# Channel shuffle on one core: one VectorE copy a tile in place of a VectorE and ScalarE pair, and a new list of tile sizes

## The chip, the cores and the metric

One core of a Trainium2 chip. The metric is the device time of one execution in microseconds (us), as a median over several executions.

## The reference

```python
# x: (16, 64, 64, 256) float32, groups = 8
x = x.reshape(batch, h, w, groups, c // groups)
x = x.transpose(0, 1, 2, 4, 3)          # inside each row of 256 channels: 8 x 32 -> 32 x 8
return x.reshape(batch, h, w, c)
```

Each of the 65,536 rows of 1 KB is permuted in itself. 67.11 MB are read and as many written; there is no arithmetic.

## The kernel before

A tile has 128 partitions, and each partition holds q consecutive rows, so "a 24 KB tile" means 24 KB a partition, 3.146 MB in all. In the memory of the chip a partition's part of a tile is one contiguous run of q KB. I call such a run a *row of the transfer* below. A transfer *lands* when its last bytes have arrived and the engine that waits for it can go on. The *plateau* is the flat rate in the middle of a run.

```python
_SIZES = [24] * 21 + [8]
_IN_BUFS = 4
_OUT_BUFS = 4
_SHARES = (("vector", 1), ("scalar", 1))
...
for q in _SIZES:
    in_tile = in_pool.tile([P, biggest * c], F32, name="in_tile")
    nc.sync.dma_start(out=in_tile[:, : q * c], in_=rows(x_flat, first, q))       # load
    out_tile = out_pool.tile([P, biggest * c], F32, name="out_tile")
    ...  # half of the tile's rows to nc.vector.tensor_copy, half to nc.scalar.copy,
         # each permuting "p (i g j)" -> "p (i j g)"
    nc.scalar.dma_start(out=rows(out_flat, first, q), in_=out_tile[:, : q * c])  # store
    first += P * q
```

Loads are issued by the SP queue, stores by ScalarE's queue. Four input and four output buffers of 24 KB take 192 KB of each partition.

## Time and profile before

| | before |
|---|---|
| time, median | 317.7 us |
| span of the profile | 316.0 us |
| VectorE / ScalarE busy | 21% / 38% |
| bytes / 432 GB/s | 310.7 us |
| first landing / first store issued | 11.04 / 16.80 us |
| last landing / last bytes | 302.35 / 313.7 us |

The page of the profile is read from its DMA row. If that is at 9 in every slice and the load and store queues together take nearly all of the sixteen DMA engines, an engine's idle time only says that it waits for data. The question for any change is then which part of the 5.3 us above the floor of 310.7 it can reach. The prediction shows the lines.

### The profile page before, as it was taken

The page shows a single profiled execution, that of the slowest core. Times are in us where ns is not written, and L with a number is a line of the kernel's source. Part 1 is how long each engine was busy: PE and PEld are TensorE (multiplying, and loading weights), DVE is VectorE, ACT ScalarE, POOL GpSimd, SP SyncE. Part 2 cuts the span into 40 slices and gives each one's busy share as a digit, 9 for nine tenths or more (in the row PEclk, how much of TensorE's full clock was granted, in tenths as well). Part 3 has the DMA queues.
Part 4 walks back from the last instruction along what each step waited for, and adds up shares of the span by engine and source line. Part 5 has one row for each costly group of instructions (what it writes and reads, how often), then busy time and mean ns, then how long its engine had stood idle before and what let it go on. Part 6 is the DMA issues. An engine that isn't in the chain of part 4 may idle for free.

```text
span 316.0 us, 236 instructions
## 1 busy us (share of the span) xinstructions
DVE 65.3 (21%) x22; ACT 118.9 (38%) x23; POOL 0.2 (0%) x4
## 2 busy tenths in 40 slices
DVE  0440321303030303113030303031220303030310
ACT  1681624425160606243351606061533426060620
POOL 0000000000000000000000000000000000000000
DMA  8999999999999999999999999999999999999996
GB/s 302 439 395 426 426 445 432 420 442 439 417 439 445 417 436 442 426 426 445 426 423 445 439 414 442 442 417 439 442 421 432 442 420 432 442 429 429 421 446 291
DMA packets 6337, 134.23 MB, mean 425 GB/s; under 512 B 704, under 2 KB 704, under 8 KB 704
## 3 DMA queue, kind: packets, MB, share of 16 engines
q1 hardware_dynamic: 3168, 67.11, 49.8%
q10 hardware_dynamic: 3168, 67.11, 49.3%
q14 instruction: 1, 0.01, 0.0%
HBM read 67.11 MB, written 67.11 MB: 425 GB/s over the span
## 4 chain that ended last, share of the span: by engine, by line
another core or an unknown queue 43%; DMA 32%; ACT 20%; ACTq 1%; issue 0%
DMA in_tile<-in_x_dram 32%; ACT out_tile L49 20%; ACTq L66 1%; ACTq L49 0%
## 5 line engine op out<-in xcount | busy, mean ns | idle before, releaser
L49 ACT COPY out_tile<-in_tile 128x3072 f32<-128x3072 f32 (+1 forms) x22 | 117.7, 5348 | 184.6 <-DMA in_tile<-in_x_dram 184.6
L51 DVE COPY out_tile<-in_tile 128x3072 f32<-128x3072 f32 (+1 forms) x22 | 65.3, 2968 | 238.3 <-DMA in_tile<-in_x_dram 238.3
L49 ACT ACT_TABLE_LOAD x1 | 1.3, 1283 | 0.7 <-PEq L84 0.7
L84 POOL MEMSET const-bfloat16-1.0<- 128x1 bf16 x1 | 0.1, 102 | 0.0
L84 POOL MEMSET const-uint8-127<- 128x1 uint8 x1 | 0.1, 102 | 0.0
L84 POOL MEMSET const-float32-1.0<- 128x1 f32 x1 | 0.1, 99 | 0.0
L84 POOL MEMSET const-float32-0.0<- 128x1 f32 x1 | 0.1, 98 | 0.2 <-issue 0.2
## 6 DMA issues: line engine op xcount, KB each, us to landing
in_tile<-in_x_dram SPq DMA_DIRECT2D x21, 3072.0 KB, 52.6
out_dram<-out_tile ACTq DMA_DIRECT2D x21, 3072.0 KB, 20.2
in_tile<-in_x_dram SPq DMA_DIRECT2D x1, 1024.0 KB, 47.9
out_dram<-out_tile ACTq DMA_DIRECT2D x1, 1024.0 KB, 10.4
```

Of the source, the lines that this page charges most:

```text
L49: nc.scalar.copy(out=dst, in_=src)
L51: getattr(nc, engine).tensor_copy(out=dst, in_=src)
L66: nc.scalar.dma_start(out=rows(out_flat, first, q), in_=out_tile[:, : q * c])
L84: nc = _bacc.Bacc("TRN2", target_bir_lowering=False, num_devices=1)
```

## The change

The intent: let stores begin earlier (small tiles first), take ScalarE out of the copying so that it only issues stores, and keep everything in program order. 44 transfers become 48. The line with `manual_schedule` is meant to keep the program order; no run has it alone (e1 has it together with the VectorE copies, e2 has neither).

```diff
-_SIZES = [24] * 21 + [8]
+_SIZES = [4, 4, 8] + [24] * 20 + [16]
...
-_SHARES = (("vector", 1), ("scalar", 1))
...
+    ctx.enter_context(tc.manual_schedule(engines=None))
...
-        at, total = 0, sum(n for _, n in _SHARES)
-        for k, (engine, n) in enumerate(_SHARES):
-            ...
-            permute(engine, out_tile[:, cols], in_tile[:, cols])
+        nc.vector.tensor_copy(
+            out=out_tile[:, : q * c].rearrange("p (i j g) -> p i j g", j=CPG, g=G),
+            in_=in_tile[:, : q * c].rearrange("p (i g j) -> p i j g", g=G, j=CPG),
+        )
```

More of the change, by code (lines that the diff above doesn't have):

```diff
@@ L43, in rows @@
         return flat[first * c : (first + P * q) * c].rearrange("(p f) -> p f", p=P)
-    def permute(engine, dst, src):
-        src = src.rearrange("p (i g j) -> p i j g", g=G, j=CPG)
-        dst = dst.rearrange("p (i j g) -> p i j g", j=CPG, g=G)
-        if engine == "scalar":
-            nc.scalar.copy(out=dst, in_=src)
-        else:
-            getattr(nc, engine).tensor_copy(out=dst, in_=src)
+    ctx.enter_context(tc.manual_schedule(engines=None))
     first = 0
@@ L57 @@
         out_tile = out_pool.tile([P, biggest * c], F32, name="out_tile")
-        at, total = 0, sum(n for _, n in _SHARES)
-        for k, (engine, n) in enumerate(_SHARES):
-            last = k == len(_SHARES) - 1
-            upto = q if last else min(q, at + -(-q * n // total))
-            if upto > at:
-                cols = slice(at * c, upto * c)
-                permute(engine, out_tile[:, cols], in_tile[:, cols])
-            at = upto
+        nc.vector.tensor_copy(
+            out=out_tile[:, : q * c].rearrange("p (i j g) -> p i j g", j=CPG, g=G),
+            in_=in_tile[:, : q * c].rearrange("p (i g j) -> p i j g", g=G, j=CPG),
+        )
         nc.scalar.dma_start(out=rows(out_flat, first, q), in_=out_tile[:, : q * c])
```

## The prediction

> **What bounds the kernel now.** I read the page from the top: busy shares first, then the DMA rows, then the waits, then windows cut at the kernel's own events.
>
> ```profile
> DVE 65.3 (21%) x22; ACT 118.9 (38%) x23; POOL 0.2 (0%) x4
> ...
> DMA  8999999999999999999999999999999999999996
> ...
> q1 hardware_dynamic: 3168, 67.11, 49.8%
> q10 hardware_dynamic: 3168, 67.11, 49.3%
> ...
> L49 ACT COPY out_tile<-in_tile 128x3072 f32<-128x3072 f32 (+1 forms) x22 | 117.7, 5348 | 184.6 <-DMA in_tile<-in_x_dram 184.6
> L51 DVE COPY out_tile<-in_tile 128x3072 f32<-128x3072 f32 (+1 forms) x22 | 65.3, 2968 | 238.3 <-DMA in_tile<-in_x_dram 238.3
> ```
>
> The two copying engines work for 21% and 38% of the span of 316.0 us, and all their other idle time ends with the landing of an input tile. The load queue (q1) and the store queue (q10) together take 49.8 + 49.3 = 99.1% of what sixteen DMA engines have. In the row of forty slices only the first and the last are below 9. So the kernel is bound by the transfers, and what is left beside them is at the two ends. The next view says how much (windows cut at the landings of tiles 0 to 3, at the last two landings and at the last bytes; the last two columns are DMA share and GB/s):
>
> ```profile
> 0.00:2.00 2.00, 0.00 (x0) 1.27 (x1) 0.20 (x4) 1.00 0.71 160
> 2.00:18.30 16.30, 3.16 (x1) 5.74 (x2) 0.00 (x0) 1.00 0.96 410
> 18.30:30.80 12.50, 3.25 (x1) 5.86 (x1) 0.00 (x0) 1.00 1.00 405
> 30.80:60.00 29.20, 6.47 (x2) 11.71 (x3) 0.00 (x0) 1.00 1.00 433
> 60.00:292.60 232.60, 48.31 (x16) 86.99 (x16) 0.00 (x0) 1.00 1.00 432
> 292.60:302.40 9.80, 3.02 (x1) 5.48 (x2) 0.00 (x0) 1.00 1.05 450
> 302.40:313.70 11.30, 1.09 (x1) 1.89 (x1) 0.00 (x0) 1.00 0.96 411
> 313.70:316.00 2.30, 0.00 (x0) 0.00 (x0) 0.00 (x0) 1.00 0.04 18
> ```
>
> In the 262 us from 30.8 on to 292.6 the rate is flat at 432 to 433 GB/s with a share of 1.00. The page gives 134.23 MB, so at 432 GB/s everything takes 134.23 / 0.432 = 310.7 us. The span is 316.0 us: **5.3 us** are all that lie above that floor. They are, each window's length times what it lacks of 432: 1.3 us before 2.0; 0.8 us in the ramp to 18.3; 0.8 us in the window where the first stores join the loads; minus 0.4 us at 292.6; 0.5 us in the store-only drain; and 2.2 us after the last bytes, while the completion comes back. These sum to 5.2 us.
>
> **What the Trainium skill says.** "DMA: Bandwidth & Descriptors", section "Where 436 GB/s comes from", derives a ceiling of 435.2 GB/s for the sixteen ports together. The trace agrees: the plateau is 432 to 433, within 1% of it. "HBM Reference", section "Specifications", says that a core streaming alone reaches about 425 GB/s, bounded by its DMA engines and not by its share of the memory; the page's mean is 425. "DMA: Bandwidth & Descriptors", section "Issuing engines are not separate DMA queues", says that transfers from different issuing engines run on the same sixteen DMA engines and interleave; the near-equal 49.8% and 49.3% fit. "VectorE: DVE Perf Modes", section on the perf-mode tier table, gives 1227 ns for an fp32 copy of 2048 elements, two elements a cycle. This trace differs for the permuting copy: by form, 1024 elements took 1095 ns and 3072 took 3058 ns on average, a slope of (3058 - 1095) / 2048 = 0.96 ns an element. That is close to one element a cycle at the clock of 0.96 GHz that the page states. The measurement decides; I use it below.
>
> **The change part by part.**
>
> *Removed: the ScalarE copies and their table load.* 22 copies, 117.7 us of busy time, and 1.3 us of table load go. None of it lies on the transfers' path: the table load ends at 2.0 us, long before the first tile lands at 11.04 us, and each copy is followed by about 9 us of waiting. Worth 0 us directly.
>
> *Moved: their share to VectorE.* Cost by the slope and the 112 ns that remain at 1024 elements: a 24 KB tile (6144 elements) 0.112 + 6144 x 0.958 ns = 6.0 us, 16 KB 4.0 us, 8 KB 2.1 us, 4 KB 1.1 us. Sum 20 x 6.0 + 4.0 + 2.1 + 2 x 1.1 = 128 us, about 41% of the span. A tile can come only every 2 x 3.146 MB / 0.432 = 14.56 us (load and store of 24 KB x 128), so VectorE has 8.5 us to spare on each. A tile is free for reloading about 6.0 us after landing instead of about 5.4 us with ScalarE. That 0.6 us is invisible, because a load takes 52.6 us from issue to landing with four input buffers: some three others lie ahead of it in the queue.
>
> *Moved: the stores.* Before, ScalarE runs its next copy ahead of the store of the previous tile, so stores leave in pairs every 29.1 us (issued at 190.88, 219.97 and 249.05 in the order of time), and one of each pair waits for a load. After, the listing of instructions has only stores on ScalarE's queue, so each leaves as its copy ends. The latency of a store should drop (20.2 us median now), but both directions share a pipe that is full already: 0 us.
>
> *Small tiles first.* Tile 0 before landed at 11.04: 0.73 us issue, 7.28 us of data (3.146 MB), 3.0 us of latency and ramp. With 0.524 MB it lands near 0.73 + 3.0 + 1.2 = 5 us, its copy ends near 6 us, and the first store is issued there instead of at 16.80 us. This looks like a gain of 10 us, but the DMA engines were not idle in those 10 us: they were loading tiles 0 to 2. Reading early and writing late, or mixing from the start, moves the same bytes. What can change is the small loss where stores join (0.8 us): there may now be two such places, the short stores at the start and, after a read-only stretch while tile 3 is awaited and copied, the first large one. I put +0.4 us on that.
>
> *Four more transfers (48 for 44), rows of 4 and 8 KB.* 2 x (0.52 + 0.52 + 1.05) = 4.2 MB move in shorter rows. Nothing here has 4 KB rows; if they run 10% below the plateau (a guess), 4.2 / 0.432 x 0.1 = about 1 us at most. I put +0.2 us.
>
> *The end.* The last tile is 16 KB: load 2.10 MB, 4.0 us copy (1.9 us before), store 4.9 us. Let it land at T. Loads and stores share until then, so tile 22 landed 9.7 us earlier; its copy took 6.0 and its store's data begins some 2 us after issue, at T - 1.7. By T it has moved 0.37 MB, and the remaining 2.78 MB last 6.4 us at full rate. The last store can start at T + 4.0 + 2 = T + 6.0. So the DMA engines have work across the last copy, with 0.4 us to spare. That is thin: I put +0.2 us on a part of a gap. The ending latency of 2.2 us stays.
>
> Sum: span 316.0 + 0.4 + 0.2 + 0.2 = 316.8 us. Against it stands a ramp that may fill better if stores join at 8 us rather than 18 (up to -1 us, I count -0.7). Span about 316.1 us. The timed median is 1.7 us above the profiled span (317.7 and 316.0), so **317.8 us**.
>
> **The rivals.**
>
> *The fill and the drain get shorter.* If the author's intent is right, starting the stores 10 us earlier saves up to 10 us: 308 us. Against it: windows 2.0 to 18.3 and 302.4 to 313.7 are busy 0.96 of the time at 410 and 411 GB/s. Even if every loss but the 1.3 us at the start and 2.2 us at the end went, the gain is 0.8 + 0.8 + 0.5 = about 2 us, 315.7. A gain of over 2% (6.4 us) exceeds the whole 5.3 us above the floor. It would need a plateau rate above 432, and the ceiling cited leaves under 1% there.
>
> *VectorE alone becomes the bound or holds stores back.* It would need more than 14.56 us a tile; 6.0 is estimated. Only if the copy of the double length were 2.4 times slower than its slope says. The form with 1024 and the one with 3072 lie on one line through a small offset, so I see nothing for it.
>
> *A gap at the end.* If the store of tile 22 runs ahead of the estimate, the DMA engines starve during the last 4.0 us copy and the 2 us of issue: at most 6 us, 323 us, more likely 1 to 2 us, 319 to 320.
>
> **Range and chances.** The floor with the fixed ends is about 310.7 + 3.5 + 1.7 = 316 us; the bad things I can name are 1 to 2 us each. The range is 315.6 to 319.8. Faster by over 2% (below 311.3) has 0.02, as it contradicts the plateau; slower by over 2% (above 324.1) 0.02, an idle end or an unforeseen slow small-row start; within 2% 0.96.
>
> **What would show it right or wrong.** VectorE should be near 128 us busy with 24 copies, 24 KB ones near 6.0 us; ScalarE near zero. The first landing should be near 5 us and the first store near 6 us. Stores should leave singly, 14.5 us apart. The plateau should stay at 432 to 433 GB/s. The windows around the last landing should show a full DMA share through the last copy. A plateau several GB/s away from 432, a share below 0.9 in mid-run, or a hole of several us before the last store would make the prediction wrong.

## The result, and the profile after

The changed kernel takes **317.62 us** (median of 6 runs, 317.02 to 317.97) against 317.66 us of the kernel before in the same rounds. The ratio is 0.9996, 95% interval 0.9983 to 1.0009: the same. Ratios here are the mean time of one kernel's fast runs over that of the other's of the same rounds, so not quite the ratio of the medians.

The page of the changed kernel, the same lines as the prediction shows of the one before:

```profile
DVE 122.2 (39%) x24; POOL 0.2 (0%) x4
...
DMA  8999999999999999999999999999999999999997
...
q1 hardware_dynamic: 3456, 67.11, 49.9%
q10 hardware_dynamic: 3456, 67.11, 49.5%
...
L49 DVE COPY out_tile<-in_tile 128x6144 f32<-128x6144 f32 (+3 forms) x24 | 122.2, 5093 | 175.9 <-DMA in_tile<-in_x_dram 175.7
```

ScalarE has left the list of busy engines and VectorE's busy time has nearly doubled (65.3 to 122.2 us), yet the DMA row is the same but for its last digit: 49.9 + 49.5 = 99.4%, against 99.1% before. The windows of the changed kernel, cut at its own landings (after the times: length, VectorE busy, GpSimd busy, clock, DMA share, GB/s):

```profile
0.00:2.00 2.00, 0.00 (x0) 0.20 (x4) 1.00 0.20 45
2.00:16.60 14.60, 4.21 (x3) 0.00 (x0) 1.00 1.03 415
16.60:25.30 8.70, 5.73 (x2) 0.00 (x0) 1.00 0.99 422
25.30:35.00 9.70, 5.72 (x1) 0.00 (x0) 1.00 1.03 432
35.00:49.40 14.40, 5.73 (x2) 0.00 (x0) 1.00 0.99 424
49.40:282.10 232.70, 91.32 (x17) 0.00 (x0) 1.00 1.00 432
282.10:294.20 12.10, 5.67 (x1) 0.00 (x0) 1.00 1.01 433
294.20:298.10 3.90, 3.86 (x1) 0.00 (x0) 1.00 1.07 460
298.10:313.40 15.30, 0.00 (x1) 0.00 (x0) 1.00 0.98 420
313.40:315.20 1.80, 0.00 (x0) 0.00 (x0) 1.00 0.03 9
```

The plateau is 432 GB/s in both. The last copy (294.2 to 298.1) has a full DMA share beside it. What differs from the kernel before lies in the windows at the two ends, and these lack about as much of 432 in sum (4.7 us here, 5.2 before; one profile of each, and the changed kernel's is of the fastest of its six runs).

The order of time on VectorE shows where the two kernels do differ (start, duration, what, and in brackets the idle time ahead of it and what ended it; so a start after such a wait is a landing):

```profile
4.12 2.32 DVE L49 COPY out_tile<-in_tile 128x1024 f32<-128x1024 f32 x2 [4.12 <-DMA in_tile<-in_x_dram]
7.89 2.02 DVE L49 COPY out_tile<-in_tile 128x2048 f32<-128x2048 f32 x1 [1.44 <-DMA in_tile<-in_x_dram]
16.63 5.70 DVE L49 COPY out_tile<-in_tile 128x6144 f32<-128x6144 f32 x1 [6.72 <-DMA in_tile<-in_x_dram]
25.27 5.75 DVE L49 COPY out_tile<-in_tile 128x6144 f32<-128x6144 f32 x1 [2.94 <-DMA in_tile<-in_x_dram]
35.03 5.71 DVE L49 COPY out_tile<-in_tile 128x6144 f32<-128x6144 f32 x1 [4.01 <-DMA in_tile<-in_x_dram]
49.38 5.73 DVE L49 COPY out_tile<-in_tile 128x6144 f32<-128x6144 f32 x1 [8.64 <-DMA in_tile<-in_x_dram]
63.95 5.73 DVE L49 COPY out_tile<-in_tile 128x6144 f32<-128x6144 f32 x1 [8.83 <-DMA in_tile<-in_x_dram]
```

The first tile lands at 4.12 us instead of 11.04, and the first store is issued at 5.26 instead of 16.80. But the 24 KB tiles do not land evenly: the gaps are 8.6, 9.8, 14.4 and 14.6 us. The trace counts what each queue moved in a gap. In the first one, 16.63 to 25.27 us (q1 are the loads, q10 the stores; packets, MB, share of the DMA engines' time):

```profile
q1 hardware_dynamic: 144, 3.15, 84.5%
q10 hardware_dynamic: 144, 0.52, 14.8%
```

The profile records each row as one packet, so the 144 packets are 128 rows and 16 of under 512 B, and this for loads and stores alike. The same count in every gap, from the DMA view of each window:

| gap (us) | loads' MB | stores' MB | stores / loads | rows of the stores running | ratio of row lengths |
|---|---|---|---|---|---|
| 8.64 | 3.15 | 0.52 | 0.17 | 4 KB | 4/24 = 0.17 |
| 9.76 | 3.15 | 1.04 | 0.33 | 8 KB | 8/24 = 0.33 |
| 14.35 | 3.00 | 3.11 | 1.04 | 24 KB | 1 |
| 14.57 | 3.15 | 3.15 | 1.00 | 24 KB | 1 |

So the two queues do not share bytes equally: they move equal numbers of rows, and short rows get a small share of the bytes. They take turns row by row. In the window 18.79 to 19.87, and in each of the next four of 1.08 us, each queue starts 16 rows, as many as there are DMA engines; a load's row takes 84.4% of the 1.08 us and a store's 14.7%, together one round:

```profile
q1 hardware_dynamic: 16, 0.39, 84.4%
q10 hardware_dynamic: 16, 0.07, 14.7%
```

The early stores crawl: issue to landing, in us, of the changed kernel by size (the last column is the median):

```profile
out_dram<-out_tile ACTq DMA_DIRECT2D x20, 3072.0 KB, 40.1
...
in_tile<-in_x_dram SPq DMA_DIRECT2D x2, 512.0 KB, 3.8
...
out_dram<-out_tile ACTq DMA_DIRECT2D x2, 512.0 KB, 16.8
```

A store of 512 KB takes 16.8 us where a load of the same size at the start takes 3.8. Large stores take 40.1 us where their median was 20.2 before: a queue has built up in front of them. None of this costs time, because the DMA engines are busy with loads meanwhile.

### The profile page after: what moved, and what is told of

Same layout as the page of the kernel before. It is cut to its first block, busy times and chain, and to the rows that moved or that the text cites. A ratio compares the mean times of both kernels' runs of the same rounds, so it can differ in the third digit from the quotient of the medians.

```text
span 315.2 us, 178 instructions
## 1 busy us (share of the span) xinstructions
DVE 122.2 (39%) x24; POOL 0.2 (0%) x4
## 3 DMA queue, kind: packets, MB, share of 16 engines
q1 hardware_dynamic: 3456, 67.11, 49.9%
q10 hardware_dynamic: 3456, 67.11, 49.5%
## 4 chain that ended last, share of the span: by engine, by line
DMA 38%; another core or an unknown queue 30%; DVE 25%; issue 0%; DVEq 0%
DMA in_tile<-in_x_dram 38%; DVE out_tile L49 25%; DVEq L49 0%
## 5 line engine op out<-in xcount | busy, mean ns | idle before, releaser
L49 DVE COPY out_tile<-in_tile 128x6144 f32<-128x6144 f32 (+3 forms) x24 | 122.2, 5093 | 175.9 <-DMA in_tile<-in_x_dram 175.7
## 6 DMA issues: line engine op xcount, KB each, us to landing
out_dram<-out_tile ACTq DMA_DIRECT2D x20, 3072.0 KB, 40.1
in_tile<-in_x_dram SPq DMA_DIRECT2D x1, 2048.0 KB, 49.9
out_dram<-out_tile ACTq DMA_DIRECT2D x1, 2048.0 KB, 16.3
out_dram<-out_tile ACTq DMA_DIRECT2D x2, 512.0 KB, 16.8
```

The source lines that it names most:

```text
L49: nc.vector.tensor_copy(out=out_tile[:, : q * c].rearrange("p (i j g) -> p i j g", j=CPG, g=G), in_=in_tile[:, : q * c].rearrange("p (i g ...
```

## The experiments

**Theory A:** the DMA plateau bounds both kernels; each part of the change is hidden or costs under 0.5 us. **Rivals:** B, the parts cancel each other. C, the copies lie on the path at the two ends. D, an early start gains and short rows or more transfers eat it. E, the time of the first store counts one for one. For the sharing: P, by row length, against Q, equal bytes. All results are in the table; "ratio" is against the kernel before in the same rounds.

| run | edit against the changed kernel | us | ratio, 95% interval |
|---|---|---|---|
| e1 | old sizes | 317.47 | 0.9995 (0.9982 to 1.0007) |
| e2 | copies split, and scheduled, as before | 317.54 | 0.9999 (0.9987 to 1.0012) |
| e3 | no copies (wrong result) | 317.70 | 1.0006 (0.9991 to 1.0021) |
| e4 | every copy twice | 318.47 | 1.003 (1.0016 to 1.0043) |
| e5 | every copy three times | 378.6 | one look |
| e6 | sizes 12, 12, 20 x 24, 8 | 317.56 | 0.9997 (0.9982 to 1.0012) |
| e7 | all 8 KB | 321.52 | 1.0123 (1.0106 to 1.014) |
| e8 | all 4 KB | 328.42 | 1.0334 (1.0319 to 1.035) |
| e9 | taper at both ends | 317.14 | 0.9983 (0.9971 to 0.9996) |
| e10 | e1, first copy three times | 317.61 | 0.9998 (0.9984 to 1.0011) |
| e11 | e1, first copy five times | 328.78 | 1.034 (1.0321 to 1.0359) |

### e1 and e2: one part alone

```diff
# e1: VectorE alone, old sizes (edit to the changed kernel)
-_SIZES = [4, 4, 8] + [24] * 20 + [16]
+_SIZES = [24] * 21 + [8]
# e2: split copies, new sizes (edit to the kernel before)
-_SIZES = [24] * 21 + [8]
+_SIZES = [4, 4, 8] + [24] * 20 + [16]
```

> One part alone: VectorE does all copies in program order, tile sizes as before (21 of 24 KB, then 8 KB). Theory A (the DMA plateau bounds both kernels, each part is hidden): 317.6 us, within 0.3% of the kernel before, 44 transfers, plateau 432 to 433 GB/s. Rival B (the two parts cancel: taking ScalarE out costs or gains, the small tiles give it back): this run and the next lie on opposite sides of 317.7 by 1 us or more.

> The other part alone: sizes 4, 4, 8, twenty of 24, 16 KB, copies still split between VectorE and ScalarE. Theory A: 317.6 us within 0.3% of the kernel before; the first landing near 4.1 us as in the changed kernel, and a store-to-landing median well above the 20.2 us of before, near 40, because the short rows of the first stores get a smaller share beside 24 KB rows. Rival B: off by 1 us or more, opposite in sign to the run with the old sizes.

Both are the same as before, and on the same side of it by 0.2 us at most. Rival B falls. The latency of the 24 KB stores, in the kernel before and in e1:

```profile
out_dram<-out_tile ACTq DMA_DIRECT2D x21, 3072.0 KB, 20.2
out_dram<-out_tile ACTq DMA_DIRECT2D x21, 3072.0 KB, 28.7
```

So it rises without any short row, when the stores no longer wait behind a copy on ScalarE's queue. In e2 the median is 31.9 us: longer, as expected, but not the 40 that I wrote down. There the copy of the next tile still runs ahead of every other store on ScalarE's queue, and the trace has both kinds: a store issued on time (69.3 us) took 40.3 us, one issued late (63.9) took 31.2.

### e3 and e4: no copies, and twice as many

```diff
# e3: store the loaded tile, eight input buffers, no output pool
-        nc.vector.tensor_copy(out=..., in_=...)
-        nc.scalar.dma_start(out=rows(out_flat, first, q), in_=out_tile[:, : q * c])
+        nc.scalar.dma_start(out=rows(out_flat, first, q), in_=in_tile[:, : q * c])
# e4 (and e5 with 3)
+        for _ in range(2):
             nc.vector.tensor_copy(out=..., in_=...)
```

> Changed kernel without copies: each tile is stored straight from where it was loaded, eight input buffers (wrong result on purpose). Theory A (transfers alone set the time): 317.0 to 317.8 us, the last store is issued about 3.9 us sooner after the last landing but queues behind the other stores, so nothing is gained. Rival C (the copies lie on the path at the ends, first copy 1.1 us plus last copy 3.9 us): about 312.5 us.

> Every copy of the changed kernel is done twice in place: VectorE near 2 x 122 = 244 us busy, 11.4 us for each 24 KB tile against 14.56 us between tiles. Theory A: 317.6 us within 0.5%; the last store, delayed by another 3.9 us, still finds stores queued ahead of it (in the changed kernel it took 16.3 us to land, of which its own data are 4.9). Rival C (copies lie on the path at the ends): at least 5 us longer, 322 or more.

With no copy at all the kernel takes 317.70 us. The transfers alone give the time, and rival C, which asked for 312.5, falls. With every copy done twice (VectorE 243.6 us busy, 77% of the span) it takes 0.3% more, some 0.9 us, where rival C asked for 5. About 0.5 us of that is there by 35 us: its first windows moved 13.8 MB by then, the changed kernel's 14.0. Where the rest lies I did not find.

### e5: where the slack of VectorE ends

> Every copy three times: 17.1 us on VectorE for a 24 KB tile against the 14.56 us in which its load and store move. Theory A says that here, and not before, VectorE becomes the bound: first landing 4.1 us, then 3 x 122.2 = 366.6 us without a break, then one store alone of some 8.5 us, span about 379 us, time about 381 us, DMA share near 0.82. If the copies were not what had slack, the step from once to twice (+0.9 us) would simply be repeated: about 319.5 us.

```profile
DVE 363.9 (97%) x72; POOL 0.2 (0%) x4
...
q1 hardware_dynamic: 3456, 67.11, 45.8%
q10 hardware_dynamic: 3456, 67.11, 42.0%
...
out_dram<-out_tile ACTq DMA_DIRECT2D x1, 2048.0 KB, 6.3
```

378.6 us, a single look, where theory A asked for about 381 (and for a DMA share of 0.82 and a last store of 8.5 us, both off). Three copies take 3 x 5.70 = 17.1 us a tile, more than the 14.56 us of its transfers, and now VectorE is at 97% while the two queues fall to 88%. Twice cost 0.9 us, three times 61 us: the slack has an edge between 11.4 and 17.1 us a tile, as the sum per tile says. The last line gives another number for later: the last store, alone in its queue, takes 6.3 us to land.

### e6: a test of the sharing, told beforehand

```diff
-_SIZES = [4, 4, 8] + [24] * 20 + [16]
+_SIZES = [12, 12] + [24] * 20 + [8]
```

> Changed kernel with sizes 12, 12, twenty of 24, 8 KB. Time by theory A 317.6 us, within 0.3%. Theory P (the DMA engines take loads and stores in turn row by row, so the share goes by row length): while stores of 12 KB rows run beside loads of 24 KB rows, loads get 24/36 of the plateau, and tiles 2 and 3 (both 24 KB) land 10.9 us apart; from about 35 us on, 14.6 us apart. Rival Q (equal share of bytes): 14.6 us apart already between tiles 2 and 3.

VectorE in order of time in this run:

```profile
...
11.14 2.97 DVE L49 COPY out_tile<-in_tile 128x3072 f32<-128x3072 f32 x1 [0.72 <-DMA in_tile<-in_x_dram]
21.61 5.67 DVE L49 COPY out_tile<-in_tile 128x6144 f32<-128x6144 f32 x1 [7.50 <-DMA in_tile<-in_x_dram]
32.53 5.71 DVE L49 COPY out_tile<-in_tile 128x6144 f32<-128x6144 f32 x1 [5.25 <-DMA in_tile<-in_x_dram]
45.84 5.74 DVE L49 COPY out_tile<-in_tile 128x6144 f32<-128x6144 f32 x1 [7.59 <-DMA in_tile<-in_x_dram]
60.32 5.73 DVE L49 COPY out_tile<-in_tile 128x6144 f32<-128x6144 f32 x1 [8.74 <-DMA in_tile<-in_x_dram]
```

Tiles 2 and 3 land at 21.61 and 32.53: 10.9 us apart, as P said to the tenth, and not 14.6. With all rows at 24 KB it is 14.5 (45.84 to 60.32). The total is 317.56 us. Rival Q falls: between the two landings the trace counts 3.15 MB of loads and 1.57 MB of stores, 128 rows of each. The times alone would fit turns of a whole transfer (eight rows on each DMA engine) as well; the windows of 1.08 us above, taken in the changed kernel, show turns of one row.

### e7 and e8: the price of short rows, made large

```diff
# e7                              # e8
+_SIZES = [8] * 64                +_SIZES = [4] * 128
+_IN_BUFS = 12; _OUT_BUFS = 12    +_IN_BUFS = 24; _OUT_BUFS = 24
```

> All 64 tiles of 8 KB rows, twelve buffers each way (the same memory), 128 transfers. It shows for 134 MB what the 4.2 MB of short rows of the changed kernel cost. Theory A (short rows cost nearly nothing): plateau 425 GB/s or more, 318 to 323 us. Rival D (the gain of an early start was eaten by short rows and four more transfers, at 10% on the 4.2 MB): plateau near 390 GB/s, 345 us or more.

> All 128 tiles of 4 KB rows, 24 buffers each way, 256 transfers. Theory A: a fixed cost a row that was too small to see, so a plateau of 415 GB/s or more and 319 to 330 us, unless too few transfers are in flight. Rival D: below 390 GB/s, 350 us or more.

The middle of the run (60 to 280 us) of the changed kernel, of e7 and of e8:

```profile
60.00:280.00 220.00, 85.58 (x15) 0.00 (x0) 1.00 1.00 433
```

```profile
60.00:280.00 220.00, 90.89 (x45) 0.00 (x0) 1.00 1.01 427
```

```profile
60.00:280.00 220.00, 96.28 (x88) 0.00 (x0) 1.00 1.03 420
```

The share stays full and the rate falls by little: 1.4% for 8 KB rows, 3% for 4 KB rows. A transfer gives each of the 16 DMA engines 128 / 16 = 8 rows (the 3456 packets of a queue, over 24 transfers and 16 engines, are nine: eight rows and a small one). So e8 has (256 - 44) x 8 = 1696 more rows an engine than the kernel before and takes 10.8 us longer, 6.4 ns a row; e7 has 672 more and takes 3.9 us longer, 5.8 ns. The change adds 4 x 8 = 32 rows an engine, so by this estimate it pays **0.2 us** for them. Rows and transfers grow together in these runs, so the price may be one of the transfer (eight rows) rather than of the row; the 0.2 us are the same. Rival D falls: there is neither a large gain nor a large price.

### e10 and e11: when does the time of the first store count?

```diff
# edit to e1; e11 has 5
+        for _ in range(3 if first == 0 else 1):
             nc.vector.tensor_copy(out=..., in_=...)
```

> Vector alone with the old sizes, the copy of tile 0 done three times, so the first store is issued near 11.1 + 3 x 5.7 = 28.2 us instead of 16.8. Theory A (the start of the stores is free as long as loads have work): the four loads that have buffers last until 3.7 + 4 x 7.28 = 32.8 us, later than 28.2, so 317.5 us within 0.3%. Rival E (a later first store lengthens the run by as much): about 329 us.

> The same with five copies of tile 0: the first store and the fifth load are issued near 11.1 + 5 x 5.7 = 39.6 us, data from about 41.4 us. Theory A: the loads run out of buffers at 32.8 us, so the DMA engines stand still for about 8.5 us and the time is about 326 us. Rival E: about 340 us. A theory that says the start never matters: 317.5 us.

In e10 the first store is issued at 27.84 us, 22.6 us later than in the changed kernel, and the time is the same, 317.61 us. In e11 it is issued at 39.54 us and the time is 328.78. Its windows:

```profile
2.00:33.00 31.00, 21.98 (x4) 0.00 (x0) 1.00 0.93 397
33.00:41.00 8.00, 7.97 (x3) 0.00 (x0) 1.00 0.18 34
41.00:60.00 19.00, 16.44 (x4) 0.00 (x0) 1.00 0.95 396
```

Between 33 and 41 us the DMA engines stand nearly still: four loads have filled the four input buffers, and the first copy has not freed one. The hole is worth 8 x (432 - 34) / 432 = 7.4 us. The start counts only from the moment when loads have nothing left to do. Theory A had put e11 at 326, with a hole of 8.5. The run is 11.2 us longer than e10: 7.4 are the hole, 1.6 lie in the window after it (19 x 36 / 432), and the rest I did not trace. Rival E, at 329 and 340 us, missed e10 by 11 and e11 by 11.

### e9: does anything beat both?

```diff
-_SIZES = [4, 4, 8] + [24] * 20 + [16]
+_SIZES = [4, 8, 16] + [24] * 19 + [16, 8, 4]
```

> Changed kernel with sizes 4, 8, 16, nineteen of 24, 16, 8, 4 KB, to see whether a taper at the end too beats both kernels. Theory A: nothing to gain beyond 1 us; 317.6 us within 0.4%, 50 transfers. By the row-by-row sharing the short last loads get little beside 24 KB stores, so they land late and the backlog of stores at the last landing shrinks below the 16 us of the changed kernel. Rival F (a short last store shortens the end by the 3.6 us that a 4 KB tile moves faster than a 16 KB tile): about 314 us.

317.14 us, ratio 0.9983 against the kernel before: 0.5 us, just clear of noise (5 runs). This is the fastest version here, though it was not run beside the changed kernel in the same rounds. As told, the short last loads land late beside 24 KB stores (the last at 308.50 us instead of 294.24), and the backlog at the end shrinks: the last store lands 4.9 us after its issue, not 16.3 as in the changed kernel. Rival F, at 314, falls. Which end the 0.5 us comes from was not separated.

## Why the prediction was right

The number was 317.8 (315.6 to 319.8) and the runs gave 317.62. That it is off by only 0.2 us is partly luck: the kernel before took 317.66, and the terms for what changes (+0.8 and -0.7) cancel. What tests the mechanism are the steps:

- **The bound: right.** The plateau at 432, nothing outside the ends to gain. e3 is the proof: without any copy, 317.70. Whether the 432 are the DMA engines' limit or the memory's, no run here tells.
- **ScalarE's work is worth nothing: right.** e1, old sizes with ScalarE out, 317.47.
- **VectorE's cost: a little too large.** 128 us predicted, 122.2 measured; 6.0 us for 24 KB, measured 5.71. My slope came from copies that ran while ScalarE copied the other half of the same tile. The first two such copies of the kernel before took 3.16 and 3.25 us; the same shape at the same place in e6, with ScalarE idle, took 2.96 and 2.97. That the engines slow each other may be the reason, but I ran nothing that isolates it. (That two sizes lie on one line is no evidence for the double length, as two points always do.) It does not touch the time: e4 and e5 bracket the edge of 14.56 us a tile (11.4 nearly free, 17.1 not).
- **"The latency of a store should drop": wrong.** Stores do leave singly, 14.5 us apart (55.1, 69.7, 84.2), but the median went from 20.2 to 40.1 us, in two steps. First, the prediction did not count the stores that are already queued when one leaves. In the kernel before, the store that left late, at 45.5 us, landed after 20.2, at 65.7; the next left at 51.2 and landed after 28.9. In e1 they leave at 36.8 and 51.4 and take 28.9 and 28.8: they land at the same times, 65.7 and 80.2. Leaving sooner only means a longer wait in the queue. Second, with the small tiles the three short stores get 0.17 to 0.33 of what the loads get, the loads run ahead, and the large stores queue from then on (28.7 to 40.1). Short rows are not the only way to this: in e10, where the first store is merely late, the median is 51.3. The conclusion drawn beside it (0 us) held, since it rests on the full pipe alone.
- **Small tiles first gain nothing: right.** Landing near 5 and store near 6 us, measured 4.12 and 5.26. e10 and e11 show the reason: a first store at 5, 17 or 28 us gives the same time; one at 39.5 costs 11 us, and the DMA engines begin to starve at 33.
- **Short rows and four more transfers: +0.2 us predicted, 0.2 us worked out from e7 and e8.** The guess of 10% for the worst case was far too high (1.4% and 3%); that the two 0.2 meet is luck, as the first was a discount on that guess.
- **The end: no gap, right, but not by a thin 0.4 us.** The last store lands 16.3 us after issue; alone it takes 6.3 (e5), so 10.0 us of other stores lie ahead of it. In e4 it is issued later and lands after 12.4 us, which leaves 6.1: just the 3.9 us of the second copy less. The prediction let the data of tile 22's store begin 2 us after its issue, as if no store were queued. It was issued at 287.8 us and landed 21.8 later, behind one that was issued at 273.2 and landed at 302.3. Such a backlog was there before the change too: the last store took 10.4 us, with 2.4 us of data. The 2 us were too much as well, since e5's 6.3 us are 4.9 of data and 1.4 of all else. The equal shares were at fault for the landing: tile 22 landed 12.2 us ahead of the last tile, not 9.7, since rows of 16 KB beside rows of 24 KB make it (2.10 + 3.15) / 0.432 = 12.1.
- **The small terms** (+0.4 for two places where stores join, -0.7 for the ramp) are below what the runs can resolve: the interval is -0.5 to +0.3 us. They stay open. Of the 2.2 us after the last bytes, which were put down to the completion, over half come later: the last store of the kernel before landed at 304.3 + 10.4 = 314.7 of 316.0.

## What to carry to other kernels

When the DMA engines are at their plateau from the first microseconds to the last, beginning stores earlier only changes the order of the bytes; before you shape tiles for a quick fill, check whether loads ever run out of buffers before the first store (here at 33 us, and the first store came at 17). Work per tile on an engine was nearly free up to the time in which the tile's bytes move (twice the copies cost 0.9 us) and costly beyond it (three times cost 61), so reckon that sum before moving work from one engine to another. Where loads and stores share the DMA engines, count shares by row length, not by bytes: here a short-row transfer beside a long-row one crawled. And a store that leaves sooner does not land sooner when others are queued ahead of it.

## What the Trainium skill lacked or had wrong

- "DMA: Bandwidth & Descriptors", section "Queues, rings and completion order", has the DMA engines switch between queues at packet granularity, but does not say what follows for the shares: here the queues took turns row by row, each with 128 rows between two landings of 24 KB tiles, beside stores of 4, 8, 12 or 24 KB rows. With stores of 12 KB rows against loads of 24 KB rows, 24 KB tiles landed 10.9 us apart, against 14.5 with equal rows; with 4 KB rows, 8.6.
- The same page, section "Rules for kernel authors", asks for at least 1 MiB a transfer for bandwidth. With three to four loads and as many stores in flight (e8: 9.9 us from issue to landing, a tile every 2.5 us), 512 KB ones (e8) kept 420 GB/s and 1 MB ones (e7) 427, against 433 for 3 MB ones.
- "VectorE: DVE Perf Modes", the perf-mode tier table: two elements a cycle for an fp32 copy. It has no row for a copy that permutes inside the partition, and no page gives a figure for one, though some warn of strides in general: here 6144 elements took 5.71 us, 0.93 ns an element, against 1227 / 2048 = 0.60 ns in the table.
